# The last token tiles of a fused decoder layer: a written-out order for the final normalisation, and earlier issue of two cache copies

## The chip, the cores and the metric

The kernel runs on one core of a Trainium2 chip. A core has TensorE (PE: matrix products into PSUM, with PEld for its weight loads), VectorE (DVE), ScalarE (ACT), GpSimd (POOL), a queue of DMA issues on SyncE (SP) and 16 DMA engines. The metric is the device time of one execution in microseconds; lower is better. Times of parts are read from one execution that was recorded by the hardware profiler; positions in it are microseconds from the start of its span.

## The reference

One layer of a hybrid decoder is computed in float32 for a prompt of 2048 positions and for 8 samples of 4 new positions each, with a cache of 2048 keys and values per sample. Attention and the spatial gate come first; the part that matters here is the end of the layer and the caches:

```python
def _rmsnorm(x, g):
    y = xf * lax.rsqrt(jnp.mean(xf * xf, axis=-1, keepdims=True) + EPS)
    return (y * g.astype(jnp.float32)).astype(x.dtype)

def _swiglu(x, g, w_gate, w_up, w_down):
    h = _rmsnorm(x, g)
    return (jax.nn.silu(h @ w_gate) * (h @ w_up)) @ w_down
...
    x = x + jnp.concatenate([att, u * gate], axis=-1) @ w_out
    x = x + _swiglu(x, norm2_g, w_gate, w_up, w_down)      # D_MODEL 1024, D_FF 2816
...
    keep = wb + T - min(WINDOW, wb + T)                    # = 4
    return x, k_all[:, keep:], v_all[:, keep:], vn         # sample caches, moved on by 4 rows
...
    y_prompt = _rmsnorm(xp, final_g)
    y_sample = _rmsnorm(xs, final_g)
```

The new sample caches are thus the old ones without their first four rows, followed by the four new rows: 2044 of 2048 rows are a plain copy from one place in DRAM to another.

## The kernel before

The prompt is cut into 16 tiles of 128 positions. After attention, the tiles go through the rest of the layer in three blocks: tiles 0 to 5, 6 to 11, and 12 to 15. The last block also carries the 32 sample rows as a fifth, smaller tile; its index is `m` = 4 in `B.rows`. A block runs the output projection, the second norm, and then 22 steps `f` over the 2816 hidden columns, 128 at a time. Each step has seven products `q` (a fast matrix product with seven instead of eight block products, with each operand split into a high and a low half, L1680 to L1682), which leave the hidden activations `hw` (`hs` for the samples). After every two steps the two hidden slices are multiplied by `w_down` and added to the block's running sums `B.acc[i]`. This is `down_unit` (L1745): per tile two halves of 512 columns, each six matmuls (L1760) into a PSUM bank and one VectorE addition into `acc` (L1762), called an eviction below. `first_downs` (L1764) does the same for the first two tiles of the last pair, slice by slice, with its evictions at L1778.

PSUM has eight banks in this part. `ps_o()` takes the next of two banks in turn, `ps_m()` the next of four; a bank can be filled again when its eviction has ended.

The order on each engine is the order in which the program emits instructions; nothing is moved afterwards, and an instruction that waits holds up all behind it on its engine. Work that should come later in the emitted order is put off with `later(n, ...)` by n ticks of a clock, and `tick()` emits what is due. So the last tiles of the last block are emitted as `down_unit` calls, with the final norm of finished tiles (`final_a`, `rms_b`, `final_b`, `final_store`) let in between:

- `final_a` (L1781) squares a tile on ScalarE with the sum of each row taken along (L1788). For the sample tile it first adds the lower half of the rows, which holds the part of the low operand halves, to the upper: a copy on ScalarE (L1785) and an addition on VectorE (L1786).
- `rms_b` (L1447) makes mean square plus epsilon on VectorE (L1450) and its root on ScalarE (L1451).
- `newton` (L140) takes the reciprocal on VectorE and one Newton step, with four small instructions for one column, five for more columns.
- `final_b` (L1792) scales the tile by the reciprocal root and by `final_g` in one VectorE instruction with three operands (L1796), called a scaling below; `final_store` issues the store (L1802, L1804).

`square_tile()` hands out two SBUF tiles in turn for the results of the squares, which nobody reads.

The caches are copied by DMAs from DRAM to DRAM, in 128 pieces of 512 KB (`pieces`, L1321). `roll(n)` (L1323) issues the next n pieces on SP's queue. The steps of the blocks call it at L2062: at q = 1 of each step in block 0, at q = 1, 3, 5 in block 1, at q = 1, 3 in block 2, each time where another step follows. What is left is issued at the very end (L2099). Between them the same queue carries the loads of prepared operands (`fr<-ab_d`, L1571) and of `w_down` (L1660), and the stores. The operands that a step's product q loads and splits (`prepare`, L1642) are used a whole step later.

Of the kernel before, what the change touches and what calls it, by code (L numbers as in the profile page):

```python
# [10 lines left out]
F32 = mybir.dt.float32  # L11
F32R = mybir.dt.float32r
AF = mybir.ActivationFunctionType
OP = mybir.AluOpType
# [5 lines left out]
P = 128  # L20
T = 2048
NT = T // P
D = 1024
# [5 lines left out]
NF = FF // P  # L29
SB = 8  # L30
ST = 4
SR = SB * ST
WB = 2048
EPS = 1e-6
# [31 lines left out]
def hymba_step(ctx: ExitStack, tc: tile.TileContext, A: dict, O: dict):  # L66
    nc = tc.nc
    sync, act, dve, pool, pe = nc.sync, nc.scalar, nc.vector, nc.gpsimd, nc.tensor
# [5 lines left out]
    pairs = ExitStack()  # L74
# [8 lines left out]
    def bank(which):  # L83

        return psum.tile([P, 512], F32, name="ps_%s%d" % ("ttoo"[which], which), tag="b%d" % which, bufs=1)

    def ps_m(which=None):

        if which is None:
            turn[3] = which = (turn[3] + 1) % 4  # L90
        return pool_["pm"].tile([P, 512], F32, name="ps_m%d" % which, tag="m%d" % which, bufs=1)

    def ps_o():
        turn[1] ^= 1
        return bank(2 + turn[1])
# [26 lines left out]
    ident = consts.tile([P, P], F32, name="ident")  # L122
# [17 lines left out]
    def newton(r, v):  # L140

        dve.reciprocal(r, r)
        if r.shape[-1] == 1:
            dve.tensor_scalar(v, v, r, r, op0=OP.mult, op1=OP.mult)  # L144
            dve.tensor_scalar(v, v, -0.5, 1.5, op0=OP.mult, op1=OP.add)
            dve.tensor_scalar(r, r, v, None, op0=OP.mult)  # L146
            return
        dve.tensor_mul(v, v, r)
        dve.tensor_mul(v, v, r)
        dve.tensor_scalar(v, v, -0.5, 1.5, op0=OP.mult, op1=OP.add)  # L150
        dve.tensor_mul(r, r, v)
# [17 lines left out]
    def pair_tile(dtype=F32R):  # L169
        return rp.tile([P, 2, 512], dtype, name="pair", tag="pair", bufs=2)  # L170
# [543 lines left out]
    for half in range(2):  # L714
        for ki, kind in enumerate(ORDER[half]):
            for gi, tiles in enumerate(GROUPS):
                start = ((half * 5 + ki) * 3 + gi) * 8
                for k in range(KD):
                    if start == 0:

                        for j in range(3):
                            n = 3 * k + j
# [7 lines left out]
                for j, tj in enumerate(tiles):  # L730
# [7 lines left out]
                    ps = lambda key=key, j=j: outs[key][j]  # L738
# [15 lines left out]
                    else:  # L754
                        layer_norm(e + 1, t, lambda t=t: zn["g", t], P)

                        f = e + 4 + (4 if tj in (4, 5) else 0)
                        at(f, "turn", gate_split, t)
                        if tj % 4 == 3:
                            g = t // 4  # L760
                            for x in range(4):
                                y = f + (2, 3, 5, 6)[x]
# [452 lines left out]
    for h in range(H):  # L1215
# [4 lines left out]
        if end:  # L1220

            x = s0 - NI
# [26 lines left out]
    for i, it in enumerate(items):  # L1249
        x, h, n = B0 + i, it["h"], it["n"]  # L1250
# [3 lines left out]
        if it["kind"] == "s":  # L1254
# [6 lines left out]
            v = min(y for y in range(x + 6, x + 14) if y not in taken)  # L1261
# [28 lines left out]
    FC = 2  # L1290
# [26 lines left out]
    def square_tile():  # L1317
        return pair_tile(F32).rearrange("p a b -> p (a b)")
# [15 lines left out]
    def later(n, fn, *args, ahead=False):  # L1334
        due[clock[0] + n, not ahead, len(seq)] = (fn, args)
        seq.append(0)

    def tick():
        clock[0] += 1
        while due and min(due)[0] <= clock[0]:  # L1340
            fn, args = due.pop(min(due))
            fn(*args)
# [311 lines left out]
    def ahead_of(f, s):  # L1654
        for fn, j in (ODD_AHEAD if f % 2 else EVEN_AHEAD).get(s, ()):
            fn(f, j)
# [5 lines left out]
    wd = {}  # L1662
# [67 lines left out]
    def hidden(B, u, zz, c):  # L1730
# [11 lines left out]
            lows.append((lo_, g[:, :, 64:], hi.bitcast(F32)))  # L1742
        return lows

    def down_unit(B, i, h):  # L1745
        tick()
        nr = P if B.rows[i] == P else 2 * SR
        for half in range(2):
            cs = slice(half * 512, (half + 1) * 512)
            ps = ps_o()  # L1750
            for z in range(FC):
                dh, dl = wd[z]
                hh, hl, hs_ = h[z]
                if B.rows[i] == P:
                    ts = slice(i * P, (i + 1) * P)
                    pairs = ((hh[:, ts], dh), (hh[:, ts], dl), (hl[:, ts], dh))
                else:
                    pairs = ((hs_, dh), (hs_, dl))
                for y, (l_, r_) in enumerate(pairs):
                    pe.matmul(ps[0:nr], l_, r_[:, cs], start=(z == 0 and y == 0),  # L1760
                              stop=(z == FC - 1 and y == len(pairs) - 1))
            dve.tensor_add(B.acc[i][0:nr, cs], B.acc[i][0:nr, cs], ps[0:nr])  # L1762

    def first_downs(B, i0, i1, h):  # L1764

        halves = [(i, half, ps) for i in (i0, i1) for half, ps in ((0, ps_o()), (1, ps_m()))]
        for z in range(FC):
            dh, dl = wd[z]
            hh, hl, _ = h[z]
            for y, (i, half, ps) in enumerate(halves):  # L1770
                if y % 2 == 0 and z:
                    tick()
                cs = slice(half * 512, (half + 1) * 512)
                ts = slice(i * P, (i + 1) * P)
                for x, (l_, r_) in enumerate(((hh[:, ts], dh), (hh[:, ts], dl), (hl[:, ts], dh))):
                    pe.matmul(ps, l_, r_[:, cs], start=(z == 0 and x == 0), stop=(z == FC - 1 and x == 2))  # L1776
                if z:
                    dve.tensor_add(B.acc[i][:, cs], B.acc[i][:, cs], ps)  # L1778
# [20 lines left out]
    def final_store(B, i, then):  # L1799
        if B.rows[i] == P:  # L1800
            t0 = (B.b0 + i) * P
            sync.dma_start(O["yp"][t0:t0 + P, :], B.acc[i])  # L1802
        else:
            sync.dma_start(O["ys"], B.acc[i][0:SR])  # L1804
        if then:
            later(1, *then)


    blocks = [Block(0, 6), Block(6, 12), Block(12, NT)]
    B = blocks[0]  # L1810

    B.banks = (2, 0, 3, 4, 5, 2)
    gain = []
# [52 lines left out]
    fl = right.enter_context(tc.tile_pool(name="fl", bufs=1, side="right", reuse_waits="tile"))  # L1866
    h = H - 1
# [155 lines left out]
    for bi, B in enumerate(blocks):  # L2023
        if bi == 0:
            first_block(B)
        else:
            next_block(B, downs, finals)
        if B.last:
            hs4 = consts.tile([P, 4, 2 * SR], F32R, name="hs4", tag="cats")
        nb = None if B.last else blocks[bi + 1]  # L2030

        part = 4 if B.nt == 6 else 2
        units = [dict(f=0, a=0, b=part), dict(f=0, a=part, b=B.nt)] + [dict(f=f, a=0, b=B.nt) for f in range(1, NF)]
        rows = list(range(len(B.rows)))
        last_h = {}

        def one(u, q):
            tick()
            product(B, u, q)
            f = u["f"]  # L2040
            if u["b"] < B.nt:
                if bi == 0 and q in (0, 2):
                    sources(B, 2, q, q + 1)
                return

            if f and q < 2:
                prepare(B, f, 7 + q)
            if f + 1 < NF:
                prepare(B, f + 1, q)
            if f + 2 < NF:  # L2050
                if bi == 0 and f:
                    if q in (0, 2):
                        sources(B, f + 2, q, q + 1)
                if bi == 0:
                    ahead_of(f + 2, q)
            elif nb:

                for s in {(0, 2): (0, 1), (0, 4): (2, 3), (1, 3): (4, 5), (1, 5): (6, 7)}.get((f + 2 - NF, q), ()):
                    load_wo(0, s, fraw)
                if f + 1 == NF and q > 0:  # L2060
                    split_wo(nb, 0, q - 1, lambda s: op_tile())
            if f + 1 < NF and q in (1, 3, 5)[:(1, 3, 2)[bi]]:  # L2062
                roll(1)

            if f % 2 == 0 and q == 6:
                split_down(f, dve if bi == 0 and f == 0 else None)
                load_down(f + 1)
            elif f % 2 == 1 and q == 3:
                split_down(f)
                if f + 1 < NF:  # L2070
                    load_down(f + 1)

        def downs_of(pair, a, b):
            for i in rows[a:b]:
                down_unit(B, i, pair)

        for n, u in enumerate(units):
            u["n"] = n
            for q in range(7):
                one(u, q)  # L2080
                if u["f"] % 2 == 0 and u["f"] > 0 and 3 <= q < 6:
                    downs_of((B.h[0], B.h[1]), *((0, 2), (2, 4), (4, 9))[q - 3])
        pair = (B.h[0], B.h[1])
        if B.last:
            first_downs(B, 0, 1, pair)
            later(1, final_a, B, 0)
            later(2, final_a, B, 1)
            for i in rows[-1:] + rows[2:-1]:
                down_unit(B, i, pair)
                later(1, final_a, B, i)  # L2090
            for _ in range(6):
                tick()
        else:

            last = ([4] if nb.last else []) + [i for i in rows if not (nb.last and i == 4)]
            downs = [lambda B=B, pair=pair: first_downs(B, last[0], last[1], pair)]
            downs += [lambda B=B, pair=pair, i=i: down_unit(B, i, pair) for i in last[2:]]
            finals = [lambda B=B, nb=nb, i=i: final_a(B, i, (load_acc, nb, i) if i < len(nb.rows) else None) for i in last]
# [116 lines left out]
```

## Time and profile before

| what | us |
| --- | --- |
| median of 3 runs (lowest, highest) | 2535.84 (2529.48, 2545.74) |
| the profiled execution | 2539.89 |
| its span | 2538.1 |
| PE busy in the span | 2452.0 (97%) |
| DVE, ACT, POOL busy | 1431.8, 1221.0, 1378.7 |
| mean granted clock of TensorE | 0.991 |
| cache copies (L1326) in the span | 128, the last issued at 2532.0 |

A row of the order in time gives start, duration, engine, line, operation, result and operands with shapes, how many instructions were merged into the row (x), and in brackets the idle time of the engine before it with what ended it. A row of the busy time by stretches gives the stretch, its length, the busy time of PE, PEld, DVE, ACT and POOL with the number of instructions, the granted clock, the busy share of the DMA engines, and the GB/s that they moved. SPq is SyncE's queue; its durations are those of issuing, not of the transfer. The profiled execution is 4.05 us slower than the median of the runs, and 1.8 us of it lie outside the span.

### The profile page before, as it was taken

To read this page: it belongs to the slowest core of one execution; us is meant where nothing else is said; L and a number is where in the kernel's file an instruction comes from. 1 tells how busy PE (TensorE), PEld (TensorE's weight loads), DVE (VectorE), ACT (ScalarE), POOL (GpSimd) and SP (SyncE) were. 2 spreads that over 40 slices of the span, in tenths; PEclk is the share of its full clock that TensorE was granted. 3 is DMA by queue.
4 is the path that set the end of the run, shared out by engine and by line. 5 is a ranking of instruction groups with operands and counts; after the bars stand their busy time and mean duration, and the time that the engine had idled before them with its cause. 6 is when DMAs were issued, how large, how long until landed. Compare 5 with 4: busy or idle time off the path is not lost. (4 is left out here: it accounts for less than half of the span.)

```text
span 2538.1 us, 38943 instructions
## 1 busy us (share of the span) xinstructions
PE 2452.0 (97%) x13598; PEld 2169.2 (85%) x13598; DVE 1431.8 (56%) x2775; ACT 1221.0 (48%) x2579; POOL 1378.7 (54%) x1078
## 2 busy tenths in 40 slices
PE   9999989999999899999999999999999999999996
PEld 7787867778888878999999988999999988999996
DVE  4379785347888866444444475444444466444445
ACT  6424344446877747545545456323323236344432
POOL 1136653133667657767767644644635434776662
PEclk9999999999999999999999999999999999999998
DMA  8864944787787674645536463653644553665553
GB/s 273 248 185 133 297 127 133 245 264 235 199 237 232 169 208 150 212 156 168 198 133 211 147 207 116 217 186 136 217 149 169 192 169 125 224 212 194 195 189 109
DMA packets 313585, 480.00 MB, mean 189 GB/s; under 512 B 25889, under 2 KB 178882, under 8 KB 307502
## 3 DMA queue, kind: packets, MB, share of 16 engines
q1 hardware_dynamic: 308428, 469.00, 57.9%
q10 hardware_dynamic: 4962, 8.51, 1.2%
q8 instruction: 108, 1.77, 0.3%
q14 instruction: 87, 0.71, 0.1%
HBM read 381.72 MB, written 165.83 MB: 216 GB/s over the span
## 5 line engine op out<-in xcount | busy, mean ns | idle before, releaser
L1621 POOL TENSOR_TENSOR op<-fr,op 128x512 fp32r<-128x512 f32 x393 | 499.2, 1299 | 278.5 <-ACT op L1617 264.7
L1682 PE MATMUL ps_m<-xh,op 128*128 128x384 f32 (+5 forms) x1932 | 610.2, 316 | 0.2
L1680 PE MATMUL ps_m<-xh,op 128*128 128x384 f32 (+5 forms) x1932 | 610.1, 316 | 0.0
L1681 PE MATMUL ps_m<-xl,op 128*128 128x384 f32 (+5 forms) x1932 | 609.2, 315 | 0.0
L1760 PE MATMUL ps_o<-dw,hw 128*128 128x512 f32 x2040 | 481.4, 391 | 5.1 <-DVE acc L1762 5.1
L1760 PEld LDWEIGHTS ps_o<-dw,hw 128*128 128x128 f32 x2040 | 380.1, 188 | 84.7 <-DVE acc L1762 8.4
L1762 DVE TENSOR_TENSOR acc<-acc,ps_o 128x512 f32<-128x512 f32 (+1 forms) x362 | 247.8, 687 | 220.5 <-PE ps_o L1760 220.4
L1680 PEld LDWEIGHTS ps_m<-xh,op 128*128 128x128 f32 x1932 | 363.8, 188 | 4.0
L1681 PEld LDWEIGHTS ps_m<-xl,op 128*128 128x128 f32 x1932 | 363.7, 188 | 3.5
L1682 PEld LDWEIGHTS ps_m<-xh,op 128*128 128x128 f32 x1932 | 363.6, 188 | 0.8 <-POOL op L1621 0.8
L1727 ACT ACTIVATE ps_t<-zn 128x384 f32<-128x384 f32 (+2 forms) x132 | 60.0, 454 | 459.4 <-DVE zn L1710 346.2
L1617 ACT ACTIVATE op<-fr 128x512 fp32r<-128x512 f32 x396 | 235.3, 623 | 19.4 <-DMA fr<-ab_d 14.1
L138 POOL TENSOR_TENSOR dw<-fd,dw 128x1024 fp32r<-128x1024 f32 x65 | 156.2, 2403 | 120.1 <-ACT dw L135 119.2
L323 PE MATMUL ps_s<-wh,xh 128*128 128x512 f32 x480 | 195.3, 407 | 6.1 <-ACT xh L135 6.0
L324 PE MATMUL ps_s<-wl,xh 128*128 128x512 f32 x480 | 190.3, 396 | 2.6 <-DVE wl L226 2.6
L325 PE MATMUL ps_s<-wh,xl 128*128 128x512 f32 x480 | 189.7, 395 | 0.0
L1737 ACT ACTIVATE hw<-ps_t 128x384 fp32r<-128x384 f32 (+2 forms) x132 | 57.7, 444 | 176.6 <-DVE ps_t L1733 175.6
L1621 POOL TENSOR_TENSOR op<-pair,op 128x512 fp32r<-128x512 f32 x63 | 81.2, 1295 | 100.2 <-ACT op L1617 96.0
L323 PEld LDWEIGHTS ps_s<-wh,xh 128*128 128x128 f32 x480 | 91.4, 190 | 35.2 <-issue 7.5
L324 PEld LDWEIGHTS ps_s<-wl,xh 128*128 128x128 f32 x480 | 91.7, 191 | 22.2 <-DVE wl L226 5.3
L325 PEld LDWEIGHTS ps_s<-wh,xl 128*128 128x128 f32 x480 | 91.2, 190 | 19.9 <-DVE xl L138 0.3
L621 POOL TENSOR_TENSOR vl<-kv,vh 100x512 fp32r<-100x512 f32 (+1 forms) x32 | 42.9, 1341 | 108.5 <-ACT vh L615 71.7
(486 smaller groups left out, 4788.1 us busy)
## 6 DMA issues: line engine op xcount, KB each, us to landing
fr<-ab_d SPq DMA_DIRECT2D x308, 256.0 KB
fd<-in_w_down_dram SPq DMA_DIRECT2D x66, 512.0 KB
out_ks_dram<-in_cache_k_dram SPq DMA_DIRECT2D x56, 512.0 KB
out_vs_dram<-in_cache_v_dram SPq DMA_DIRECT2D x56, 512.0 KB
ab_d<-fr SPq DMA_DIRECT2D x88, 256.0 KB
raw<-in_w_in_dram SPq DMA_DIRECT2D x72, 256.0 KB
qk_d<-pair SPq DMA_DIRECT2D x64, 256.0 KB
ab_d<-pair SPq DMA_DIRECT2D x63, 256.0 KB
```

The lines of the kernel that those rows point to most:

```text
L138: (eng_lo or pool).tensor_sub(lo, src, hi.bitcast(F32))
L323: pe.matmul(o[j], xh[:, k, :], wh, start=(k == 0), stop=False)
L324: pe.matmul(o[j], xh[:, k, :], wl, start=False, stop=False)
L325: pe.matmul(o[j], xl[:, k, :], wh, start=False, stop=(k == KD - 1))
L1617: act.activation(ops[f, j][0], ab[f][j], AF.Copy)
L1621: (pool if f or j else dve).tensor_sub(lo_, ab[f][j], hi.bitcast(F32))
L1680: pe.matmul(out, wh[:, ks], xh[:, :, k], start=(k == 0), stop=False)
L1681: pe.matmul(out, wh[:, ks], xl[:, :, k], start=False, stop=False)
L1682: pe.matmul(out, wl[:, ks], xh[:, :, k], start=False, stop=(k == 3))
L1727: act.activation(g, c, AF.Silu)
L1760: pe.matmul(ps[0:nr], l_, r_[:, cs], start=(z == 0 and y == 0), stop=(z == FC - 1 and y == len(pairs) - 1))
L1762: dve.tensor_add(B.acc[i][0:nr, cs], B.acc[i][0:nr, cs], ps[0:nr])
```

## The change

The end of the last block no longer goes through `final_a` and the clock. A function `last_rows` emits it in one order of its own. The order of the matmuls stays: tiles 0 and 1 in `first_downs`, the sample tile, tile 2, tile 3. `down_unit` is cut into `down_half`, so that other work can stand between the two halves of a tile, and the bank is handed in: tile 3 takes banks of `ps_m()` where it took those of `ps_o()`. A dummy root on ScalarE is emitted ahead of everything. The roots are taken together for tiles 0 and 1, and for tile 2 and the sample tile (in columns of one small tile, which a memset fills first because the sample has only 32 rows), and alone for tile 3. The addition of the sample's two halves goes from VectorE to GpSimd. All five scalings are VectorE instructions as before; each is followed directly by its store. The sample tile's scaling is the last.

In the steps of the last block, the first two (f = 0 and 1) issue three cache copies instead of two, the third at q = 5.

```diff
+    def down_half(B, i, h, half, ps):
+        nr = P if B.rows[i] == P else 2 * SR
+        cs = slice(half * 512, (half + 1) * 512)
+        for z in range(FC):
...
+        dve.tensor_add(B.acc[i][0:nr, cs], B.acc[i][0:nr, cs], ps[0:nr])
+
     def down_unit(B, i, h):
         tick()
-        nr = P if B.rows[i] == P else 2 * SR
         for half in range(2):
...
+            down_half(B, i, h, half, ps_o())
...
+    def last_rows(B, h):
+
+        sa, va, ra, sb, vb, rb_ = (fl.tile([P, 4], F32, name="s1", tag="s1", bufs=6) for _ in range(6))
+
+        def squares(i, s_, c):
+            n = B.rows[i]
+            act.activation(square_tile()[:n], B.acc[i][:n], AF.Square, accum_out=s_[:n, c:c + 1])
+
+        def roots(s_, v, r, a, b):
+            dve.tensor_scalar(v[:, a:b], s_[:, a:b], 1.0 / D, EPS, op0=OP.mult, op1=OP.add)
+            act.activation(r[:, a:b], v[:, a:b], AF.Sqrt)
+
+        def scaled_row(i, r):
+            n = B.rows[i]
+            x = B.acc[i][:n]
+            dve.scalar_tensor_tensor(x, x, r[:n], gain[0][:n], op0=OP.mult, op1=OP.mult)
+            final_store(B, i, None)
+
+        m = len(B.rows) - 1
+        act.activation(ra[:, 3:4], ident[:, 0:1], AF.Sqrt)
+        dve.memset(sb, 1.0)
+        first_downs(B, 0, 1, h)
+        squares(0, sa, 0)
+        squares(1, sa, 1)
+        down_unit(B, m, h)
+        roots(sa, va, ra, 0, 2)
+        tick()
+        y = square_tile()
+        act.activation(y[0:SR], B.acc[m][SR:2 * SR], AF.Copy)
+        pool.tensor_add(B.acc[m][0:SR], B.acc[m][0:SR], y[0:SR])
+        newton(ra[:, 0:2], va[:, 0:2])
+        down_half(B, 2, h, 0, ps_o())
+        scaled_row(0, ra[:, 0:1])
+        down_half(B, 2, h, 1, ps_o())
+        squares(2, sb, 0)
+        squares(m, sb, 1)
+        scaled_row(1, ra[:, 1:2])
+        down_half(B, 3, h, 0, ps_m())
+        roots(sb, vb, rb_, 0, 2)
+        newton(rb_[:, 0:2], vb[:, 0:2])
+        down_half(B, 3, h, 1, ps_m())
+        squares(3, sb, 2)
+        scaled_row(2, rb_[:, 0:1])
+        roots(sb, vb, rb_, 2, 3)
+        newton(rb_[:, 2:3], vb[:, 2:3])
+        scaled_row(3, rb_[:, 2:3])
+        scaled_row(m, rb_[:, 1:2])
...
-            if f + 1 < NF and q in (1, 3, 5)[:(1, 3, 2)[bi]]:
+            if f + 1 < NF and q in (1, 3, 5)[:(1, 3, 3 if f < 2 else 2)[bi]]:
                 roll(1)
...
         if B.last:
-            first_downs(B, 0, 1, pair)
-            later(1, final_a, B, 0)
-            later(2, final_a, B, 1)
-            for i in rows[-1:] + rows[2:-1]:
-                down_unit(B, i, pair)
-                later(1, final_a, B, i)
-            for _ in range(6):
-                tick()
+            last_rows(B, pair)
```

`down_half` has the loop that `down_unit` had, with the bank as an argument.

More of the change, by code (lines that the diff above doesn't have):

```diff
@@ L1743, in hidden @@
         return lows
+    def down_half(B, i, h, half, ps):
+        nr = P if B.rows[i] == P else 2 * SR
+        cs = slice(half * 512, (half + 1) * 512)
+        for z in range(FC):
+            dh, dl = wd[z]
+            hh, hl, hs_ = h[z]
+            if B.rows[i] == P:
+                ts = slice(i * P, (i + 1) * P)
+                pairs = ((hh[:, ts], dh), (hh[:, ts], dl), (hl[:, ts], dh))
+            else:
+                pairs = ((hs_, dh), (hs_, dl))
+            for y, (l_, r_) in enumerate(pairs):
+                pe.matmul(ps[0:nr], l_, r_[:, cs], start=(z == 0 and y == 0),
+                          stop=(z == FC - 1 and y == len(pairs) - 1))
+        dve.tensor_add(B.acc[i][0:nr, cs], B.acc[i][0:nr, cs], ps[0:nr])
     def down_unit(B, i, h):
         tick()
-        nr = P if B.rows[i] == P else 2 * SR
         for half in range(2):
[L1749 to L1762, printed above, removed]
+            down_half(B, i, h, half, ps_o())
     def first_downs(B, i0, i1, h):
```

## The prediction

> **What bounds the kernel now.** I read the page first, then busy time by stretches of the last block, then the end in the chain of waits and in order of time. The first fence has part 1 of the page and, from the busy time by stretches (columns: the stretch, its length, then PE, PEld, DVE, ACT, POOL busy, granted clock, share of the DMA engines, GB/s), one steady stretch and two of the end.
>
> ```profile
> PE 2452.0 (97%) x13598; PEld 2169.2 (85%) x13598; DVE 1431.8 (56%) x2775; ACT 1221.0 (48%) x2579; POOL 1378.7 (54%) x1078
> ...
> 2186.00:2440.00 254.00, 254.00 (x1693) 234.82 (x1693) 123.28 (x274) 103.39 (x233) 167.07 (x119) 1.00 0.58 198
> ...
> 2524.00:2531.00 7.00, 0.00 (x0) 0.00 (x0) 6.07 (x16) 1.44 (x4) 0.00 (x0) 0.54 0.46 169
> ...
> 2537.00:2538.10 1.10, 0.00 (x0) 0.00 (x0) 0.00 (x0) 0.00 (x0) 0.00 (x0) 0.50 0.00 0
> ```
>
> TensorE is full up to the last rows (254.00 of 254.00 us in the long stretch). At the end VectorE carries the work (6.07 of 7.00 us), and from 2531.0 DMAs alone run. The change touches this end, 26 us of 2538, and moves two DMAs. So no outcome near 1% (25 us), about what a measurement of this kernel can tell from no change, is in sight; the question is a few us.
>
> The chain of waits in that stretch (start, us, what), then the end in order of time:
>
> ```profile
> 2513.20 1.28 ACT L1451
> 2514.49 0.21 ACT s L1451
> 2514.72 1.07 ACT pair L1785
> 2515.81 1.21 DVE acc L1786
> ```
>
> ```profile
> 2510.67 1.06 ACT L1788 ACTIVATE pair<-acc 128x1024 f32<-128x1024 f32 x1 [3.42 <-DVE acc L1778]
> ...
> 2512.95 3.06 PE L1760 MATMUL ps_o<-dw,hw 128*128 128x512 f32 x12
> ...
> 2513.72 0.14 DVE L1450 TENSOR_SCALAR s<-s 128x1 f32<-128x1 f32 x1
> ...
> 2517.68 3.01 PE L1760 MATMUL ps_o<-dw,hw 128*128 128x512 f32 x12 [1.67 <-DVE acc L1762]
> ...
> 2520.40 1.26 DVE L1762 TENSOR_TENSOR acc<-acc,ps_o 128x512 f32<-128x512 f32 x2
> ...
> 2525.80 0.13 DVE L1450 TENSOR_SCALAR s<-s 128x1 f32<-128x1 f32 x1
> 2525.97 0.20 ACT L1451 ACTIVATE s<-s 128x1 f32<-128x1 f32 x1 [4.18 <-DVE s L1450]
> 2526.08 1.04 ACT L1788 ACTIVATE pair<-acc 128x1024 f32<-128x1024 f32 x1
> 2526.20 0.16 DVE L142 RECIPROCAL s<-s 128x1 f32<-128x1 f32 x1 [0.27 <-ACT s L1451]
> ...
> 2527.02 0.19 ACT L1788 ACTIVATION_READ_ACCUMULATOR pair<-acc 128x1 f32 x1
> 2527.15 1.29 DVE L1796 SCALAR_TENSOR_TENSOR acc<-acc,s,final_g 128x1024 f32<-128x1024 f32 x1
> 2528.35 0.15 DVE L1450 TENSOR_SCALAR s<-s 128x1 f32<-128x1 f32 x1
> ...
> 2529.71 1.28 DVE L1796 SCALAR_TENSOR_TENSOR acc<-acc,s,final_g 128x1024 f32<-128x1024 f32 x1
> 2531.02 0.33 SPq L1802 DMA_DIRECT2D out_yp_dram<-acc  x1
> 2531.41 1.21 SPq L1326 DMA_DIRECT2D out_vs_dram<-in_cache_v_dram  x2
> ```
>
> Pieces: a table load and root hold ScalarE from 2513.20; behind them the sample's copy (L1785), its add on VectorE (L1786), and only then the eviction of tile 2, for which tile 3's matmuls wait (PE starts at 2517.68). VectorE then works off evictions, five Newton chains and five scalings until 2530.99; the last store and two leftover cache copies go out behind that, and the span ends at 2538.1: 7.1 us of tail.
>
> **The change, part by part.** Steps read from the rows: TENSOR_SCALAR to root 0.17 (2525.80 to 2525.97), root to RECIPROCAL 0.23, narrow Newton chain to the scaling 0.95 (2526.20 to 2527.15), scaling to next instruction 1.20, an eviction 0.68 by itself (L1440 below) and 0.6 to the next instruction (two take 1.26), a square with its read-out 1.13 (2526.08 to 2527.21), from one engine to the next about 0.04 (the root ends at 2526.17, the reciprocal starts at 2526.20). A two-column Newton chain has five instructions; the nearest is three columns wide:
>
> ```profile
> 26.48 0.18 DVE L142 RECIPROCAL rstd<-rstd 128x3 f32<-128x3 f32 x1 [1.35 <-ACT rstd L157]
> ...
> 27.48 0.17 DVE L250 TENSOR_SCALAR rstdn<-rstd 128x3 f32<-128x3 f32 x1
> ```
>
> so 1.00 from reciprocal to the instruction behind it.
>
> *Early dummy root and memset.* The table load (1.28) goes ahead of tile 0's squares, into the 3.42 us that ScalarE stands idle before 2510.67; the squares, copies and later roots show no second load. Price nothing; if that cover were gone it would cost its 1.28 again, no more than today.
>
> *PE.* Order of tiles 0, 1, sample, 2, 3 is kept. Tile 2 starts at 2512.95 as before; tile 3 in other banks doesn't wait for tile 2's evictions, follows at about 2515.7, and is done near 2518.7 where it was 2520.7. VectorE needs it later than that (below), so by itself this is worth nothing.
>
> *Sample add on POOL.* The copy starts 0.23 behind the root, as today: TENSOR_SCALAR 2513.72, root 2513.89, copy 2514.12, POOL 1.09 later (2514.72 to 2515.81) at 2515.21. No 32x1024 add of POOL is in the trace; the nearest rows, grouped by shape (mean ns behind the busy us):
>
> ```profile
> L138 POOL TENSOR_TENSOR dw<-fd,dw 128x1024 fp32r<-128x1024 f32 x65 | 156.2, 2403 | 120.1 <-ACT dw L135 119.2
> L385 POOL TENSOR_TENSOR pair<-pair,lnb 32x512 f32<-32x512 f32 x1 | 1.3, 1296 | 1.4 <-ACT pair L384 1.4
> ```
>
> Rows of partitions don't matter, width does: 2.40 (upper bound 2 x 1.296 = 2.59, lower the 1.21 of VectorE's own add). POOL is busy 2515.21 to 2517.61, beside VectorE. Is it really beside? These rows are of VectorE and POOL at the turns of the blocks:
>
> ```profile
> 1509.58 2.55 POOL L138 TENSOR_TENSOR wol<-fr,wol 128x512 fp32r<-128x512 f32 x2 [5.58 <-ACT wol L135]
> 1509.69 0.68 DVE L1440 TENSOR_TENSOR acc<-acc,ps_t 128x512 f32<-128x512 f32 x1
> 1511.22 2.00 DVE L1796 SCALAR_TENSOR_TENSOR acc<-acc,s,final_g 128x1024 f32<-128x1024 f32 x1
> 1513.14 0.68 DVE L1417 TENSOR_TENSOR raw<-xl,xh 128x512 f32<-128x512 f32 x1
> ...
> 2090.61 3.49 POOL L138 TENSOR_TENSOR wol<-fr,wol 128x512 fp32r<-128x512 f32 x2 [3.09 <-ACT wol L135]
> 2091.16 1.79 DVE L1417 TENSOR_TENSOR raw<-xl,xh 128x512 f32<-128x512 f32 x1
> ```
>
> The same scaling takes 2.00 when it meets POOL and 1.28 otherwise; L1417 takes 1.79 instead of 0.68, and POOL's two take 3.49 instead of 2.55. The eviction from PSUM (L1440) isn't slowed. So VectorE with two SBUF operands and POOL take turns. How long is the wait? 0.72 and 1.11 are measured, against POOL instructions of 1.3 us; in the first case POOL had 0.91 left (until 2512.13). I take the whole rest of the POOL instruction. Tile 0's scaling comes up at 2515.72 (root 2513.89, reciprocal 2514.12, chain 1.00, eviction 0.6) and waits to 2517.61: 1.9 us. The low end is 0, were POOL not to matter; a gain is excluded, as nothing on VectorE gets shorter by it. The Trainium skill (SBUF — State Buffer, section "SBUF: two separate sides") states that VectorE with two SBUF inputs and GpSimd share a port pair as an exclusive lock, held for the whole instruction, whoever starts first; by it the sum has 1.9, by the measured 0.72 taken as a flat price it would end 1.2 us earlier.
>
> *VectorE's order.* From 2517.61: scaling 0 to 2518.81; eviction 2b, its sums there at 2519.49; scaling 1 from 2519.41; eviction 3a from 2520.61 to 2521.29. ScalarE squares tile 2 from 2519.53 and the sample from 2520.68 to 2521.81. The joint root of the two is queued on VectorE behind eviction 3a, and waits for that square: 2521.86, root 2522.03, reciprocal 2522.26, chain to 2523.26. Behind this wait are eviction 3b and everything after it: 3b 2523.26 to 2523.94, scaling 2 from 2523.86, square of tile 3 to 2525.11, its TENSOR_SCALAR 2525.15, reciprocal 2525.55, scaling 3 from 2526.50, sample's scaling from 2527.70 to 2528.99. Last VectorE instruction: 2530.99 today, 2529.0 then: 2.0 us. (Without the lock all of it is 1.9 earlier.)
>
> *Stores and copies.* Today two 512 KB copies lie behind the last store. The change gives the last block three copies a step in its first two steps, 44 instead of 42; with one in each of block 0's 21 steps and three in each of block 1's that is 21+63+44 = 128, all of them, and none remains for the end. What a store alone needs to land: the row load that reuses an acc tile waits for its store (last row: total, times, longest wait):
>
> ```profile
> 2101.91 0.34 SPq L1802 DMA_DIRECT2D out_yp_dram<-acc  x1
> 2104.56 0.33 SPq L1370 DMA_DIRECT2D acc<-in_x_prompt_dram  x1
> ...
> SPq L1370 <- DMA out_yp_dram<-acc: 7.4, 3, 2.8
> ```
>
> 2.65 us for 512 KB, an upper bound for the sample's 128 KB that is now last. Issued at 2529.04 it lands by 2531.7; nothing moves today from 2537.0 to the end of the span, so 1.1 more: 2532.8. Tail 3.8 in place of 7.1: 3.3 us. SP has only the five stores in that order, each behind its scaling, so the in-line stores delay nothing else.
>
> *Copies in the first steps.* They pass SP's queue between loads of operands and of w_down. Each keeps the queue 0.5 to 0.6 us (two are 1.21) and about 1.6 us of all DMA engines (512 KB at 320 GB/s). These stretches, and the first wait of ScalarE on a load there, show the cover:
>
> ```profile
> 1580.00:1600.00 20.00, 20.00 (x136) 20.00 (x136) 7.08 (x19) 11.12 (x23) 18.33 (x13) 1.00 0.81 285
> ...
> 2166.00:2170.00 4.00, 4.00 (x34) 4.00 (x33) 2.58 (x8) 3.64 (x11) 4.00 (x3) 1.00 0.98 320
> ...
> 2182.00:2186.00 4.00, 4.00 (x24) 3.53 (x23) 2.06 (x3) 0.00 (x0) 0.00 (x0) 1.00 0.18 68
> ...
> 2164.53 1.06 ACT L135 ACTIVATE dw<-fd 128x1024 fp32r<-128x1024 f32 x1 [2.25 <-DMA fd<-in_w_down_dram]
> ```
>
> The DMA engines are full there, but PE is too (4.00 of 4.00), though ScalarE already waits 2.25 us for a load: operands are split one step (seven products) ahead of their use. Some 3.3 us of delay are made good by 2186, where DMA stands at 0.18. Block 1 has three copies a step from its start, and PE 20.00 of 20.00. I take nothing; the bounds are 0 and, if each load behind a copy waited for the copy to land (at most 5.0 us, from the second one's issue at about 2532.0 to 2537.0) and PE for the load, 10 us.
>
> Sum against the profiled execution: 2.0 + 3.3 = 5.3 us of 2539.89 (span 2538.1 and 1.8 around it): 2534.6. That execution is 4.05 above the median of the runs, 2535.84; the same 5.3 off the median gives **2530.5**.
>
> **Rivals.** (1) *No lock*: POOL's add costs VectorE nothing; 1.9 us more is won, 2528.6. For it: L1440's 0.68 beside POOL, and spans on POOL are rough. Against: the scaling's own 2.00. (2) *The tail stays*: the end waits for a store's landing whatever lies behind it, so 7.1 us again and 2.0 won: 2533.8. For it: the 2.65 is from another place, and no row shows the last store's own landing; against: two copies of 1.6 us of DMA each do lie behind it. (3) *Slower*: the copies in the first steps are paid by PE, 10 us at the upper bound, less 5.3: 2540.5. For it: DMA at 0.98 and the 2.25 us wait; against: block 1. It decides once PE loses more than 5.3 us around 2160 to 2190; a smaller loss only eats the gain. (4) *It does nothing*: VectorE's new order has as much waiting as the old, and the copies ended no later than the store: 2535.8. For it: three root trips through ScalarE remain; against: 3.0 us of work leave VectorE (L1786's 1.21; five Newton chains of 0.95 against two of 1.00 and one of 0.95).
>
> **How the numbers follow.** Forecast 0.60, no lock 0.15, tail stays 0.12, nothing 0.07, slower 0.06. The runs before lie from 6.4 below to 9.9 above their median, more than the cases differ; the range takes the forecast less 7.5 (that scatter, with some of the no-lock case) and plus 9.5 (scatter, and the slower cases): 2523 to 2540. No case reaches 25 us: within 1% 0.97, faster by more 0.01, slower by more 0.02.
>
> **What would show it.** Tile 3's matmuls without the 1.67 us wait, done near 2518.7 (times counted as before); a table load ahead of the squares; tile 0's scaling at some 3.2 us instead of 1.28 beside a POOL add of 2.4; the last VectorE instruction near 2529.0; no copy after the last store, and the span's end 3 to 4 us behind VectorE. PE still full from 2150 to 2190, with ScalarE's waits for loads there 1 to 3 us longer. A gap of PE there, or a tail of 7 us, makes the forecast wrong.

## The result, and the profile after

The changed kernel's median is 2529.49 us (2524.16 to 2542.51, 22 runs) against 2536.47 us (2529.48 to 2545.74, 22 runs) of the kernel before. The ratio is 0.9979, with a 95% interval of 0.9969 to 0.9988: 5.3 us less (3.0 to 7.9), and 7.0 by the two medians. The two agree within 1%, and the changed kernel is the faster one.

The profiled execution of the changed kernel is a late one: 2542.51 us, span 2540.7, longer than the profiled execution before. So positions in the two can't be compared as they stand. The next rows are, of the kernel before and then of the changed one, the group of one of the three matmul lines of the fast products (L1680; name, count, shortest, median and longest in ns, first and last start in us):

```profile
L1680 PE MATMUL ps_m<-xh,op x1932: 254/334/368, 983.5 to 2505.3; 128*128 128x384 f32 x118, 128*128 128x272 f32 x59, 128*128 128x256 f32 x6, 128*128 128x192 f32 x5
```

```profile
L1680 PE MATMUL ps_m<-xh,op x1932: 254/334/368, 992.3 to 2514.2; 128*128 128x384 f32 x118, 128*128 128x272 f32 x59, 128*128 128x256 f32 x6, 128*128 128x192 f32 x5
```

The first product stands at 983.5 us before and at 992.3 after. These 8.8 us arose ahead of that product, in parts of the layer that the change doesn't touch; from the first product to the last it is 1521.8 and 1521.9 us. I therefore measure the end from one point that both kernels have: the first matmul of the last `first_downs`.

```profile
2505.64 0.86 PE L1776 MATMUL ps_o<-dw,hw 128*128 128x512 f32 x3
```

This is the kernel before; the changed kernel's rows in order of time follow, from the same point on (its lines: L1778 `first_downs`, L1757 the other tiles' matmuls, L1759 evictions, L1817 squares, L1820 and L1821 the roots, L1826 scalings, L1830 the dummy root, L1839 the sample's copy, L1840 GpSimd's addition):

```profile
2514.56 0.86 PE L1778 MATMUL ps_o<-dw,hw 128*128 128x512 f32 x3
...
2516.26 1.28 ACT L1830 ACT_TABLE_LOAD   x1
...
2521.87 3.02 PE L1757 MATMUL ps_o<-dw,hw 128*128 128x512 f32 x12
...
2523.94 0.68 DVE L1759 TENSOR_TENSOR acc<-acc,ps_o 128x512 f32<-128x512 f32 x1
2524.20 2.38 POOL L1840 TENSOR_TENSOR acc<-acc,pair 32x1024 f32<-32x1024 f32 x1 [7.55 <-ACT pair L1839]
...
2524.54 3.12 DVE L1826 SCALAR_TENSOR_TENSOR acc<-acc,s,final_g 128x1024 f32<-128x1024 f32 x1
2524.73 2.88 PE L1757 MATMUL ps_m<-dw,hw 128*128 128x512 f32 x12
...
2528.18 1.27 DVE L1826 SCALAR_TENSOR_TENSOR acc<-acc,s,final_g 128x1024 f32<-128x1024 f32 x1
...
2530.57 0.17 DVE L1820 TENSOR_SCALAR s<-s 128x2 f32<-128x2 f32 x1 [0.52 <-ACT pair L1817]
...
2534.02 0.20 ACT L1821 ACTIVATE s<-s 128x1 f32<-128x1 f32 x1 [0.22 <-DVE s L1820]
...
2535.21 2.47 DVE L1826 SCALAR_TENSOR_TENSOR acc<-acc,s,final_g 128x1024 f32<-128x1024 f32 x2
2537.70 0.33 SPq L1806 DMA_DIRECT2D out_ys_dram<-acc  x1
```

Here ScalarE's table load comes ahead of the squares; tile 3's matmuls (2524.73) follow tile 2's (2521.87) with no wait; the scaling of tile 0 takes 3.12 us while GpSimd adds; VectorE waits 0.52 for the sample's square; its last two scalings end at 2537.68; the last store is issued at 2537.70, and the span ends 3.0 us later.

From the same point, in every kernel of this study, each row from one profiled execution (us; the tail is what lies between VectorE's last instruction and the end of the span, and as the span is printed to a tenth, the last two columns are good to about 0.05):

| kernel | PE ends | VectorE ends | span ends | tail behind VectorE |
| --- | --- | --- | --- | --- |
| before | 15.05 | 25.35 | 32.46 | 7.11 |
| changed | 13.05 | 23.12 | 26.14 | 3.02 |
| order only | 13.04 | 23.12 | 29.74 | 6.62 |
| copies only | 15.07 | 25.37 | 28.95 | 3.58 |
| no addition | 13.05 | 21.29 | 24.29 | 3.00 |
| memset in its place | 13.04 | 21.29 | 24.28 | 2.99 |
| addition on VectorE | 13.05 | 22.41 | 25.38 | 2.97 |
| two additions on GpSimd | 13.05 | 23.56 | 26.60 | 3.04 |
| 12 copies early | 13.04 | 23.12 | 26.16 | 3.04 |
| 18 copies early | 13.05 | 23.13 | 26.11 | 2.98 |
| early fold | 14.06 | 20.72 | 23.70 | 2.98 |

The end repeats to a few hundredths where a kernel's end is the same (rows "changed", "12 copies early", "18 copies early"), while whole executions of one kernel scatter over 18 us. Two executions in a slow state, 3015.61 us of the kernel before and 7687.27 us of the early fold, count neither in that nor in any ratio. So questions of a microsecond are read from this table, and the timed runs say whether the total follows.

### The profile page after: what moved, and what is told of

It is laid out like the page before. It is cut to its first block, busy times and chain, and to the rows that moved or that the text cites. A ratio compares the mean times of both kernels' runs of the same rounds, so it can differ in the third digit from the quotient of the medians.

```text
span 2540.7 us, 38936 instructions
## 1 busy us (share of the span) xinstructions
PE 2459.1 (97%) x13598; PEld 2174.5 (86%) x13598; DVE 1432.3 (56%) x2767; ACT 1221.2 (48%) x2578; POOL 1381.4 (54%) x1079
## 5 line engine op out<-in xcount | busy, mean ns | idle before, releaser
L1680 PE MATMUL ps_m<-xh,op 128*128 128x384 f32 (+5 forms) x1932 | 610.2, 316 | 0.0
L1757 PE MATMUL ps_o<-dw,hw 128*128 128x512 f32 x2028 | 478.3, 391 | 3.5 <-DVE acc L1759 3.5
L1757 PEld LDWEIGHTS ps_o<-dw,hw 128*128 128x128 f32 x2028 | 378.0, 188 | 82.2 <-DVE acc L1759 6.4
L1759 DVE TENSOR_TENSOR acc<-acc,ps_o 128x512 f32<-128x512 f32 (+1 forms) x360 | 246.8, 687 | 220.8 <-PE ps_o L1757 220.6
L1680 PEld LDWEIGHTS ps_m<-xh,op 128*128 128x128 f32 x1932 | 363.8, 188 | 4.0
L138 POOL TENSOR_TENSOR dw<-fd,dw 128x1024 fp32r<-128x1024 f32 x65 | 156.2, 2403 | 121.2 <-ACT dw L135 119.9
```

The lines of the kernel that those rows point to most:

```text
L138: (eng_lo or pool).tensor_sub(lo, src, hi.bitcast(F32))
L1680: pe.matmul(out, wh[:, ks], xh[:, :, k], start=(k == 0), stop=False)
```

## The experiments

### Each half of the change alone

`e1_order_only` is the changed kernel with the old copies:

```diff
-            if f + 1 < NF and q in (1, 3, 5)[:(1, 3, 3 if f < 2 else 2)[bi]]:
+            if f + 1 < NF and q in (1, 3, 5)[:(1, 3, 2)[bi]]:
```

> The changed kernel with its last rows' order, but two copies a step in the last block as before, so two copies are left for the very end. Measured from the first matmul of the last first_downs, the kernel before ends VectorE's work at 25.35 us and the span at 32.46 us, the changed kernel at 23.12 and 26.14. My theory (the order and the copies each win their own part): VectorE ends near 23.1 as in the changed kernel, and the tail behind it is again 6.5 to 7.1 us, so the span ends near 30; total 2 to 2.7 us under the kernel before. Rival (the copies ended no later than the store, all of the gain is the order): the span ends near 26 to 27, total 5 to 6 us under the kernel before.

`e2_copies_only` is the kernel before with the new line of these two, and nothing else.

> The kernel before with only the two copies moved into the last block's first two steps. My theory: VectorE ends at 25.3 us from the first matmul of the last first_downs, the tail shrinks from 7.1 to 3.0 to 3.8 us (a whole tile's 512 KB store is last here), the span ends near 28.5 to 29.2; total 3.3 to 4 us under the kernel before. Rival (a store's own landing takes as long): tail 6 to 7 us, total within 1 us of the kernel before. Rival (PE pays for the copies in the first steps): PE shows gaps between the start of the last block's products and its third step, and the total is equal or above.

The end of the order alone in order of time, VectorE's last row and the queue's:

```profile
2526.11 2.47 DVE L1826 SCALAR_TENSOR_TENSOR acc<-acc,s,final_g 128x1024 f32<-128x1024 f32 x2
...
2528.61 0.33 SPq L1806 DMA_DIRECT2D out_ys_dram<-acc  x1
2528.99 1.15 SPq L1326 DMA_DIRECT2D out_vs_dram<-in_cache_v_dram  x2
```

And that of the copies alone, the queue's last row (two stores, the second behind the scaling) and VectorE's:

```profile
2523.89 2.90 SPq L1802 DMA_DIRECT2D out_yp_dram<-acc  x2
...
2525.14 1.28 DVE L1796 SCALAR_TENSOR_TENSOR acc<-acc,s,final_g 128x1024 f32<-128x1024 f32 x1
```

With the order alone VectorE is done at 2528.58, the two copies go out behind the last store, and the span ends at 2535.2: the tail stays at 6.62. With the copies alone the last store is issued at 2526.46 (the second of the two, behind VectorE's end at 2526.42) and the span ends at 2530.0: 3.58. The ends are 2.72 and 3.51 us earlier than before, 6.23 together; both at once give 6.32. So the parts add to within 0.1 us, and the copies are the larger one. The timed ratios agree: 0.9989 (0.9976 to 1.0002), 2.8 us, for the order; 0.9984 (0.9971 to 0.9998), 4.1 us, for the copies. The first of these intervals includes no change, so the order's own part rests on the profile.

### GpSimd's addition and the scaling beside it

`e3_no_add` leaves the addition out:

```diff
-        pool.tensor_add(B.acc[m][0:SR], B.acc[m][0:SR], y[0:SR])
```

> The changed kernel without GpSimd's addition of the sample tile's two halves (left out: the lower halves' part of the sample rows is missing from their result). In the changed kernel the scaling of tile 0 takes 3.12 us, GpSimd's add runs from 2524.20 to 2526.58 beside it. My theory (the scaling waits for the whole rest of GpSimd's instruction): the scaling takes 1.28 us, and VectorE ends 1.8 to 1.9 us earlier, near 21.3 us from the first matmul of the last first_downs. Rival (the 3.12 us come from something else, such as the store queue or the eviction beside it): the scaling stays near 3.1 and VectorE's end near 23.1.

The scaling of tile 0, and the eviction behind it:

```profile
2514.00 1.28 DVE L1826 SCALAR_TENSOR_TENSOR acc<-acc,s,final_g 128x1024 f32<-128x1024 f32 x1
2515.19 0.68 DVE L1759 TENSOR_TENSOR acc<-acc,ps_o 128x512 f32<-128x512 f32 x1
```

1.28 us, and VectorE's end moves from 23.12 to 21.29: the addition costs 1.83 us at the end, though it isn't on VectorE.

`e9_memset` keeps GpSimd busy at the same place with an instruction that writes SBUF and reads none:

```diff
-        pool.tensor_add(B.acc[m][0:SR], B.acc[m][0:SR], y[0:SR])
+        pool.memset(y, 0.0)
```

> The changed kernel with a memset of a scratch tile on GpSimd in place of the addition (left out: the lower halves' part of the sample rows). It asks whether it is GpSimd's being busy, or its reading of SBUF, that holds up VectorE's scaling. The Trainium skill (SBUF — State Buffer, section SBUF: two separate sides) says that a VectorE instruction with two SBUF inputs contends only with a GpSimd instruction that reads SBUF. By that, and if the memset lies beside the scaling, the scaling takes 1.28 us and VectorE ends near 21.3 us from the first matmul of the last first_downs, as with no addition. Rival (any GpSimd instruction with SBUF holds the scaling): the scaling is longer than 1.28 by what is left of the memset.

```profile
2515.24 0.95 POOL L1840 MEMSET pair<- 128x1024 f32 x1 [7.64 <-ACT pair L1839]
2515.61 1.28 DVE L1826 SCALAR_TENSOR_TENSOR acc<-acc,s,final_g 128x1024 f32<-128x1024 f32 x1
```

The memset runs until 2516.19, the scaling starts 0.37 us into it and takes 1.28 all the same. So it isn't GpSimd's being busy that holds VectorE up; the addition, with its two operands in SBUF, does. With the rule that the expectation quotes from the Trainium skill (SBUF — State Buffer, section "SBUF: two separate sides"), the trace agrees: 1.28 us beside the memset, 3.12 beside the addition.

`e5_two_adds` puts a second addition behind the first:

```diff
+        pool.tensor_add(y[0:SR], y[0:SR], y[0:SR])
```

> The changed kernel with a second addition of the same size on GpSimd right behind the first (its result is not used). It asks how the two engines take turns. My theory (VectorE waits for the instruction that runs, and is next): the scaling of tile 0 takes 3.1 us as in the changed kernel, the second add stands behind it for 1.3 us, and scaling 1 may wait again for up to 1.3 us; VectorE ends 0 to 1.3 us later than 23.1. Rival (GpSimd keeps its turn while it has work): the scaling of tile 0 takes 5.5 us and VectorE ends 2.4 us later, near 25.5.

```profile
2517.74 2.38 POOL L1840 TENSOR_TENSOR acc<-acc,pair 32x1024 f32<-32x1024 f32 x1 [7.73 <-ACT pair L1839]
2518.09 3.13 DVE L1826 SCALAR_TENSOR_TENSOR acc<-acc,s,final_g 128x1024 f32<-128x1024 f32 x1
2520.20 2.75 POOL L1841 TENSOR_TENSOR pair<-pair 32x1024 f32<-32x1024 f32 x1
2521.13 0.68 DVE L1759 TENSOR_TENSOR acc<-acc,ps_o 128x512 f32<-128x512 f32 x1
2521.73 2.31 DVE L1826 SCALAR_TENSOR_TENSOR acc<-acc,s,final_g 128x1024 f32<-128x1024 f32 x1
```

The scaling of tile 0 waits for the first addition only (3.13), then runs, though GpSimd has its second addition ready; the eviction from PSUM (0.68) passes beside the second addition; scaling 1 waits for the rest of that one (2.31). So GpSimd doesn't keep its turn while it has work. VectorE ends 0.44 us later: 0.6 of the second wait's 1.0 us fell where VectorE would have waited for the sample's square anyhow.

How long the second addition waits for the scaling can't be read from its 2.75 us, since no run shows that addition alone; it is 0.37 us longer than the first, where 1.3 was expected. That GpSimd waits as well is shown at a turn of the blocks of the kernel before: one of its instructions with two operands in SBUF, 1.28 us long otherwise (L138, 128x512), starts at 1500.52, 0.63 us before a scaling ends, and takes 1.78.

VectorE's wait follows one measure in five rows. A scaling that starts beside such a GpSimd instruction (L138 or the addition) ends 1.08 to 1.10 us after that instruction's end, whatever was left of it: 0.30 us (at 2100.50 of the kernel before), 0.91 (at 1511.22 there), 1.22 and 2.03 (here) and 2.04 (the changed kernel). So the wait is the rest of GpSimd's instruction less some 0.2 us.

`e4_add_on_vector` takes the addition back to VectorE, ahead of the scaling of tile 0:

```diff
-        pool.tensor_add(B.acc[m][0:SR], B.acc[m][0:SR], y[0:SR])
...
         down_half(B, 2, h, 0, ps_o())
+        dve.tensor_add(B.acc[m][0:SR], B.acc[m][0:SR], y[0:SR])
         scaled_row(0, ra[:, 0:1])
```

> The changed kernel with that addition on VectorE, ahead of tile 0's scaling. My theory: the add takes 1.21 us, the scaling 1.28, together 0.6 us less than the 3.12 us that the scaling now takes, and VectorE ends 0.5 to 0.7 us earlier than in the changed kernel, near 22.5 us from the first matmul of the last first_downs. Rival (the add on GpSimd does free VectorE, at least in part): VectorE ends later than 23.1, by up to 1.2 us.

```profile
2506.70 1.21 DVE L1842 TENSOR_TENSOR acc<-acc,pair 32x1024 f32<-32x1024 f32 x1
2507.84 1.27 DVE L1826 SCALAR_TENSOR_TENSOR acc<-acc,s,final_g 128x1024 f32<-128x1024 f32 x1
```

VectorE ends at 22.41, 0.71 us earlier than with GpSimd's help; the ratio to the kernel before is 0.9969 (0.9957 to 0.9981). So at the end of the profile, handing the work to GpSimd cost more than doing it; the timed interval overlaps that of the changed kernel and can't tell the two apart.

### More copies in the first steps

`e6_copies_12` and `e8_copies_18` issue two and three copies at each of the three places in the last block's first two steps, where the changed kernel issues one (`e6` shown):

```diff
-                roll(1)
+                roll(2 if nb is None and f < 2 else 1)
```

> The changed kernel with two copies at each of the three places in the last block's first two steps: 12 copies there instead of 6 (the last steps then have none). It doubles the load that the rival 'slower' fears. My theory (operands are loaded a step ahead, so delays of some us are made good): PE has no gap between the last block's first product and its third step, total as the changed kernel, 5 us under the kernel before, within 1.5 us. Rival (the first steps are at their limit): PE stands idle for 3 to 10 us between about 20 and 60 us after the block's first product, and the total is at or above the kernel before.

> Three copies at each of the three places in the last block's first two steps: 18 there, where the changed kernel has 6. With 12 the last block's products took 371.7 us instead of 369.4, and PE stood 1.8 us, after ScalarE had waited 6.1 us for a load of w_down behind the copies (2.25 in the kernel before). My theory (there is a cover of some 7 us, beyond which each copy costs PE its whole transfer of 1.6 us): six more copies cost nearly 9.8 us more, the last block's products take 378 to 382 us. Rival (the loss grows with the copies from the first on, in proportion): 2.3 us for 6 more copies, so 4.6 us for 12 more, 374 us.

In rows of the order in time, the longest wait of ScalarE for a load of w_down in these steps (in brackets), first of the changed kernel, then of 12 copies and of 18, the latter two with PE's longest wait:

```profile
2174.09 1.06 ACT L135 ACTIVATE dw<-fd 128x1024 fp32r<-128x1024 f32 x1 [2.90 <-DMA fd<-in_w_down_dram]
```

```profile
2169.17 1.06 ACT L135 ACTIVATE dw<-fd 128x1024 fp32r<-128x1024 f32 x1 [6.08 <-DMA fd<-in_w_down_dram]
...
2173.98 0.40 PE L1682 MATMUL ps_m<-xh,op 128*128 128x272 f32 x1 [1.48 <-POOL op L1621]
```

```profile
2169.17 1.06 ACT L135 ACTIVATE dw<-fd 128x1024 fp32r<-128x1024 f32 x1 [11.28 <-DMA fd<-in_w_down_dram]
...
2172.00 0.56 PE L1680 MATMUL ps_m<-xh,op 128*128 128x272 f32 x1 [5.50 <-ACT hs L1741]
```

ScalarE stands behind one late load, and with it the splitting of the next operands that stand behind it in its order. The last block's products, first to last, take 369.4 us in the kernel before and in the changed one, 371.7 with 12 copies and 378.4 with 18. The first two added copies cost PE nothing, the next six 2.3 us, the six after them 6.7. This is a cover that is used up, not a price in proportion (that would have been 374 for 18); per copy the last six cost 1.1 us, less than the 1.6 that I took, and part of that is a lower clock (last section). For 12 copies neither side of the expectation came out: PE does stand idle, but for 1.8 us, less than the rival's 3 to 10. By the middle value of the total, ratio 0.9995 (0.9981 to 1.0009), nearly all of the gain is gone; a loss of 2.3 us would leave some 3, which the interval includes.

### A version without the addition in the tail

`e7_fold_early` folds the sample tile's lower half into the upper in the block's last step, after its first product, and runs its last product with three terms on 32 rows instead of two on 64 (the product of the two low parts is then left out there, as it is for the whole tiles):

```diff
+    def fold(B):
+        m = len(B.rows) - 1
+        y = square_tile()
+        act.activation(y[0:SR], B.acc[m][SR:2 * SR], AF.Copy)
+        dve.tensor_add(B.acc[m][0:SR], B.acc[m][0:SR], y[0:SR])
+        folds.append(m)
...
+            elif folded:
+                pairs = ((hs_[:, 0:SR], dh), (hs_[:, 0:SR], dl), (hs_[:, SR:2 * SR], dh))
...
+        down_half(B, m, h, 0, ps_o())
+        roots(sa, va, ra, 0, 2)
+        newton(ra[:, 0:2], va[:, 0:2])
+        down_half(B, m, h, 1, ps_o())
+        squares(m, sb, 1)
         scaled_row(0, ra[:, 0:1])
```

The evictions of tile 2 go behind scaling 0, that of tile 3's second half ahead of the second Newton chain.

> A version that may beat both: the sample tile's lower half is folded into the upper one step earlier, in the block's last step, beside PE's work; its last product then runs with three terms on 32 rows, so no addition is left in the tail (four more matmuls on PE, 0.9 us). The joint roots come a place earlier on VectorE, the eviction of tile 3's second half goes ahead of the second Newton chain. My theory (VectorE's own work and its waits for the roots bound the tail): no scaling takes more than 1.3 us, VectorE ends near 20.5 to 21.5 us from the first matmul of the last first_downs instead of 23.1, the span near 23.5 to 24.5; total 1.6 to 2.6 us under the changed kernel and 7 to 8 under the kernel before. Rival (PE becomes the bound of the tail by its four more matmuls): VectorE ends at 22.2 us or later.

> The early fold once more, beside the changed kernel on one chip. In the profiles its span ended 2.4 us sooner from the same anchor (23.70 against 26.14 us). My theory: its median is 1.5 to 3.5 us under the changed kernel's in this set. Rival (the fold costs the block's last steps what it saves at the end): no difference.

> The changed kernel as it is, timed beside the early fold. Expected 5 to 6 us under the kernel before, 1.5 to 3.5 us above the early fold; VectorE ends at 23.1 us and the span at 26.1 us from the first matmul of the last first_downs.

Its rows at the scalings of tiles 0 and 1, of the first of these runs:

```profile
2510.34 1.27 DVE L1838 SCALAR_TENSOR_TENSOR acc<-acc,s,final_g 128x1024 f32<-128x1024 f32 x1
...
2511.54 1.30 DVE L1771 TENSOR_TENSOR acc<-acc,ps_o 128x512 f32<-128x512 f32 x2
...
2512.76 1.28 DVE L1838 SCALAR_TENSOR_TENSOR acc<-acc,s,final_g 128x1024 f32<-128x1024 f32 x1
```

No scaling waits. PE ends 1.0 us later (14.06), VectorE 2.40 us earlier (20.72, and 20.71 in the second run), the span at 23.70 and 23.66 instead of 26.14. The last block's products take 369.4 us as before, so the fold costs PE nothing there. Timed, the fold has 0.9970 (0.9955 to 0.9985) and 0.9969 (0.9957 to 0.9981) of the kernel before, and the changed kernel beside it 0.9975 (0.9965 to 0.9986): medians 2526.53 and 2528.71 us. By this ratio the changed kernel is 6.3 us under the kernel before, a little more than the 5 to 6 expected. The fold beats the kernel before clearly; that it beats the changed kernel rests on the 2.4 us of the profiles, as the timed intervals overlap.

## Why the prediction was right, point by point

The forecast was 2530.5 us, 5.3 under the kernel before; measured 2529.49, and 5.3 by the ratio. That these two agree to a tenth is luck: the interval goes from 3.0 to 7.9, and the profile shows a larger gain (below). Its steps, with positions from the common point (prediction less 2505.64):

- **Early root.** As predicted: the load at 2516.26 lies ahead of the squares, and the roots behind it take 0.20.
- **PE.** Predicted to end near 13.1, measured 13.05, without the wait.
- **The addition on GpSimd.** Predicted 2.40 us, measured 2.38. The wait: 3.2 us for the scaling predicted, 3.12 measured, and 1.9 us at VectorE's end against 1.83 when the addition is left out. Taking the whole rest of GpSimd's instruction, not the shorter 0.72 us that one row showed, was right but for 0.2 us; that row was short because only 0.91 us of GpSimd's instruction was left. (That instruction ended at 1512.13; the prediction's 2512.13 is a slip.)
- **VectorE's order.** Its end was predicted at 23.35, measured 23.12: 2.23 us won for 2.0. The wait for the sample's square (0.52) and the three trips to ScalarE came where they were put. Early root, other banks, joint roots and the new sequence were only run together, so which of them brings the order's gain isn't shown.
- **The tail.** This is the term that was mis-sized: 3.8 us predicted, 3.02 measured, so 4.1 us won for 3.3. The prediction took the landing of a whole tile's 512 KB, 2.65 us, as the landing of the sample's 128 KB, and added 1.1 in which nothing moves. In the changed kernel bytes move for 1.7 us from the last store's issue, and from 2539.4 to the end, 1.3 us, none do. With 512 KB last (copies only) the tail is 3.58, near the prediction's sum; the 0.6 less is put down to the smaller last store, which no run changes by itself. The 2.65 was in part a lucky choice: at the same turn of the blocks another load waited 6.2 us for a store.
- **Copies in the first steps.** Taken at nothing; the last block's products take 369.4 us before and after, and PE is full. ScalarE's longest wait for a load grew from 2.25 to 2.90, not by the 1 to 3 us that I named.
- **The sum.** From the common point 6.32 us are won, where 5.3 was forecast; the timed interval holds both.

The rivals: *no lock* fell with the run without the addition. *The tail stays* fell with the copies alone, *it does nothing* with the profiles of both halves. *Slower* had the mechanism right (a load of w_down behind the copies, ScalarE in front of the operands) and fell on its size: the cover was enough for two more copies, and was gone with eight more. Of the 22 executions one lies outside the range, the profiled one, 2542.51 us, whose first product came late; of the twelve timed beside the fold one does, 2522.84 us, just below it.

## What to carry to other kernels

Work that is handed to an idle engine can hold up the engine it was taken from: look in the trace for rows of one instruction that are longer beside the other engine, and for which operands, before moving it. Transfers that nothing depends on belong neither behind the last store nor in a stretch where loads already end waits; a place with cover takes some of them for nothing, and from a certain number on each costs. Where executions scatter by more than the change is worth, measure from an event that both kernels share.

## What was not expected of the hardware

Nearly all of the scatter between executions comes before the first product of block 0: it stood between 976.3 and 992.3 us in the thirteen profiles, while from there to the first product of the last block it was 1150.4 to 1152.5 us. What makes the first part vary was not tried.

With 18 copies the last block's products took longer by more than PE's wait. The busy time by stretches around it (columns as in the prediction):

```profile
2161.50:2176.50 15.00, 8.35 (x53) 7.84 (x52) 3.02 (x9) 6.50 (x15) 6.24 (x6) 0.81 1.02 381
```

PE was idle for 6.65 us, and the granted clock was 0.81 in this stretch and 0.97 in the next. The last block's products took 9.0 us more, with 2.35 us more of PE's busy time than the kernel before (371.75 against 369.40). In finer stretches the clock is 0.99 from 2166.50, where PE's wait begins, to 2170.70, then 0.50 until 2177.50, and 1.00 behind that: it fell inside the wait of 5.50 us, which ended at 2172.00. With 12 copies, where PE's longest wait was 1.48 us, it stayed at 1.00. That the wait causes the lower clock is argued from this; no run changes the one without the other.
